# FFN second projection of two layers in float32: the first weight quarter loaded once, the residual loaded seven steps later, eight result sums at other products

## The chip, the cores and the metric

One core of a Trainium2 chip. The metric is device time in microseconds of one execution of the whole program, as the median of three runs. Five engines run beside each other, each through its own instructions in the order in which they were written: TensorE (PE, matmuls; its weight loads are listed as PEld), VectorE (DVE), ScalarE (ACT), GpSimd (POOL) and SyncE (SP). Here SP only starts transfers (DMA), and POOL starts a few more, among them all those that add to their destination. Sixteen DMA engines carry the transfers of both queues.

## The reference

Two layers on 1024 positions of width 1024, float32. The first is a mixer of three branches, the second a mixer with attention followed by a gated MLP with a short convolution. Only the end of that MLP matters here:

```python
z = h @ w_up                       # 1024 x 1024 times 1024 x 5632
...                                # causal convolution of 3 taps over the positions
gate, val = jnp.split(zc, 2, axis=-1)
return (jax.nn.silu(gate) * val) @ w_down      # 1024 x 2816 times 2816 x 1024
```

The result is added to the residual `x` (1024 x 1024), and that is the output.

## The kernel before

All matmuls work on float32 values split into a high and a low part (`hilo`, lines 164 to 166: ScalarE rounds the value to the high part, VectorE subtracts to get the low part); a product of two values is three matmuls (`mm3`, line 206): high by high, high by low, low by high.

The gated activations G lie in memory as 22 tiles of 128 channels by 1024 positions (`G_sp`). The second projection (`down`, from line 1964) multiplies them by `w_dn`, 22 tiles of 128 channels by 1024 outputs. It is written as a 2 x 2 block product with seven products instead of eight. The three dimensions are halved: the positions and the outputs into `lo` and `hi` of 512, the channels into tiles f = 0 to 10 (weights `W1`, G kept in tiles `g11`, `g21` for the two halves of the positions) and 11 to 21 (weights `W2`, G loaded as `g`). The products are numbered 1 to 7 and run in the order 1, 5, 2, 6, 7, 3, 4. Each takes 11 steps, one for each f, so there are 77 units (`units`, line 1970); unit u belongs to product `units[u][0]`. One unit is four blocks of 128 positions (b = 0 to 3) with three matmuls each, accumulated in four PSUM banks. Products 1, 2, 7 and 4 use banks 0 to 3, where 2 adds on 1 and 4 adds on 7; products 5, 6 and 3 use banks 4 to 7.

The left operand x of a unit is one of the G tiles, or S, which holds for each f a running sum of G blocks (one VectorE sum for each unit of products 5, 6 and 3; product 7 forms its sum in `g11`). The right operand y is a quarter of the weights, 128 x 512 for each f, or a sum of quarters in T. T is made by transfers: in product 5 SP loads `W1[:, lo]` into it and POOL starts a transfer that adds `W1[:, hi]` (`more`, line 1975); in products 6 and 4 POOL adds further quarters. Product 7 does the same in six tiles `t3`. For products 1, 2 and 3 the quarter comes into a ring of four tiles `yr`.

The order around this is written out by hand in `step` (line 2105). Before the matmuls of unit u it issues:
- `prep(u + 3)`: the sum, and both splits into `xh`, `xl`, `yh`, `yl`, in rings of four buffers each, so that a preparation needs the buffers that unit u - 1 used;
- `load_sum(u + 9)`: the transfers that make a sum of weights;
- `load(u + 7)`: `yr` for products 1, 2 and 3, and `g` (a ring of twelve tiles in A1) for products 5, 2, 3 and 4;
- in units 13 to 20 one eighth of the residual, `x`, 512 KB;
- in unit 4 of each product, the result tasks of the product before are put into the queue `bgq`; every step takes two tasks from it. A task is one sum on VectorE over 128 x 512 (a copy on ScalarE for product 1) or one store of 128 x 512 to the output.

`opening` (line 1978) runs one slot ahead of the last two slots of the first projection's end and loads G of f = 0 to 3. `rings` (line 1986) runs at that end: it opens the rings, loads units 0 to 6 and prepares 0 to 2. `rest`, in the step of unit 0, loads G of f = 4 to 10 (line 2001) in memory that the first projection used. The last G tile, f = 21, is stored by POOL (line 1909), and POOL's adding transfers come behind that in its queue.

The results of a block b are combined with four output tiles: `t11`, `t12`, `t21`, `t22` are the parts of `x` for the two halves of positions and outputs, `p1` is a copy of product 1, and `w` is product 5 less `p1`, less product 6. In the trace T and x are in tiles named B, S, `g`, `p1` and `w` in tiles named A. All `self.tt` calls are line 159.

Of the kernel before, what the change touches and what calls it, by code (L numbers as in the profile page):

```python
# [106 lines left out]
class Kernel:  # L107
# [1856 lines left out]
    def down(self):  # L1964


        nc, I = self.nc, self.I
        st = {"g": 0}
        half = NF // 2
        units = [(p, f) for p in (1, 5, 2, 6, 7, 3, 4) for f in range(half)]  # L1970
        LOAD, SUM, PREP, LATE = 7, 9, 3, 4
        lo, hi = slice(0, H), slice(H, 2 * H)
        fetch = nc.sync.dma_start

        def more(t, w):
            nc.gpsimd.dma_start(t, w, accum_op=ALU.add)

        def opening():
            st["T"], st["S"] = (self.big(t, F).rearrange("p k (h c) -> p (k h) c", h=2)
                                for t in ("B1", "A0"))  # L1980
            for f in range(4):
                t = st["TS"[f % 2]][:, 12 + f // 2 * 2:14 + f // 2 * 2]
                st["G", f] = t
                fetch(t, self.G_sp[f].rearrange("p (h t) -> p h t", h=2))

        def rings():
            self.right.close()
            self.right = ExitStack()
            st["ring"] = self.right.enter_context(
                self.pool("gd", side="right", reuse_waits="tile"))  # L1990
            for u in range(4):
                load(u)
            for u in range(PREP):
                prep(u)
                load(u + 4)

        def rest():
            self.reopen("cd")
            for f in range(4, half):
                t = st["G", f] = self.c1.tile([P, 2, H], F, name="g%d" % f)  # L2000
                fetch(t, self.G_sp[f].rearrange("p (h t) -> p h t", h=2))
            st["T3"] = [self.c1.tile([P, H], F, name="t3_%d" % i) for i in range(6)]
            st["A1"] = self.big("A1", F, KVN)
            st["p1"] = st["A1"][:, 0:2048].rearrange("p (b c) -> p b c", b=4)
            st["w"] = st["A1"][:, 2048:4096].rearrange("p (b c) -> p b c", b=4)

        def load(u):
            if u >= len(units):
                return
            p, f = units[u]  # L2010
            G2, W1, W2 = self.G_sp[half + f], I["w_dn"][f], I["w_dn"][half + f]
            T, S = st["T"][:, f], st["S"][:, f]
            y = T
            if p == 7:
                y = st["T3"][u % 6]
            elif p in (1, 2, 3):
                y = st["ring"].tile([P, H], F, tag="yr", name="yr", bufs=4)
                fetch(y, {1: W1[:, lo], 2: W2[:, lo], 3: W2[:, hi]}[p])
            g = None
            if p in (5, 2, 3, 4):  # L2020
                st["g"] += 1
                o = 4096 + st["g"] % 12 * H
                g = st["A1"][:, o:o + H]
                fetch(g, G2[:, hi if p in (5, 4) else lo])
            st["in", u] = g, y

        def load_sum(u):

            if u >= len(units):
                return  # L2030
            p, f = units[u]
            W1, W2 = I["w_dn"][f], I["w_dn"][half + f]
            T = st["T"][:, f]
            if p == 5:
                fetch(T, W1[:, lo])
                more(T, W1[:, hi])
            elif p in (6, 4):
                more(T, W2[:, hi if p == 6 else lo])
            elif p == 7:
                t = st["T3"][u % 6]  # L2040
                fetch(t, W1[:, hi])
                more(t, W2[:, hi])

        def prep(u):
            if u >= len(units):
                return
            p, f = units[u]
            g, y = st.pop(("in", u))
            S, (g11, g21) = st["S"][:, f], (st["G", f][:, i] for i in range(2))
            if p == 5:  # L2050
                self.tt(S, g21, g, ALU.subtract)
            elif p == 6:
                self.tt(S, S, g11, ALU.subtract)
            elif p == 7:
                self.tt(g11, g11, g21, ALU.subtract)
            elif p == 3:
                self.tt(S, S, g, ALU.add)
            src = g11 if p in (1, 7) else S if p in (5, 6, 3) else g
            out = []
            for x, n in ((src, "x"), (y, "y")):  # L2060
                t = [st["ring"].tile([P, H], R, tag=n + c, name=n + c, bufs=PREP + 1) for c in "hl"]
                self.hilo(*t, x)
                out.append(t)
            st["op", u] = out

        def macs(u, banks):
            p, f = units[u]
            (xh, xl), (yh, yl) = st["op", u]
            first = f == 0 and p not in (2, 4)
            for b in banks:  # L2070
                ts = slice(b * P, (b + 1) * P)
                self.mm3(st[p][b], (xh[:, ts], xl[:, ts]), (yh, yl), first, f == half - 1,
                         skip_group_check=True)

        def results(p):

            x, tasks = st["x"], []

            def store(t, cs):
                nc.sync.dma_start(self.out[t][:, cs], x[:, t, cs])  # L2080

            for b in range(4):
                ps, p1, w = st[p][b], st["p1"][:, b], st["w"][:, b]
                t11, t12, t21, t22 = x[:, b, lo], x[:, b, hi], x[:, 4 + b, lo], x[:, 4 + b, hi]
                add = lambda o, i, op=ALU.add: tasks.append(lambda: self.tt(o, o, i, op))
                if p == 1:
                    tasks.append(lambda p1=p1, ps=ps: nc.scalar.copy(p1, ps))
                elif p == 5:
                    tasks.append(lambda w=w, ps=ps, p1=p1: self.tt(w, ps, p1, ALU.subtract))
                elif p == 6:  # L2090
                    add(w, ps, ALU.subtract)
                    add(t21, ps)
                    add(t21, p1)
                    add(t12, w)
                    add(t22, w)
                else:
                    o, op, t, cs = {2: (t11, ALU.add, b, lo), 7: (t22, ALU.subtract, 4 + b, hi),
                                    3: (t12, ALU.add, b, hi), 4: (t21, ALU.add, 4 + b, lo)}[p]
                    add(o, ps, op)
                    tasks.append(lambda t=t, cs=cs: store(t, cs))  # L2100
            if p == 6:
                tasks[:] = tasks[0::5] + tasks[1::5] + tasks[2::5] + tasks[3::5] + tasks[4::5]
            return tasks

        def step(u):
            p, f = units[u]

            def pre():
                if u == 0:
                    sets = [self.pair() for _ in range(4)]  # L2110
                    banks = [pr[:, i * H:(i + 1) * H] for pr in sets for i in range(2)]
                    for q in range(1, 8):
                        st[q] = banks[0:4] if q in (1, 2, 7, 4) else banks[4:8]
                    rest()
                prep(u + PREP)
                load_sum(u + SUM)
                load(u + LOAD)
                if u == half + 2:
                    st["x"] = self.big("B0", F)
                if half + 2 <= u < half + 10:  # L2120
                    t = u - half - 2
                    nc.sync.dma_start(st["x"][:, t], self.x2_sp[t])
                if u >= half + LATE and f == LATE:
                    self.bgq.extend(results(units[u - half][0]))
                for _ in range(2):
                    if self.bgq:
                        self.bgq.popleft()()

            def mm():
                if u == len(units) - 2:  # L2130
                    for b in range(4):
                        macs(u, (b,))
                        macs(u + 1, (b,))
                elif u < len(units) - 1:
                    macs(u, range(4))
                else:
                    for task in results(p):
                        task()

            self.slots.append(Slot(pre=pre, mm=mm, name="dn%d.%d" % (p, f)))  # L2140

        self.slots[-2].pre = opening
        self.slots[-1].tail = rings
        for u in range(len(units)):
            step(u)
# [83 lines left out]
```

## Time and profile before

| | us |
|---|---|
| median of 3 runs | 2711.1 (2710.7 to 2712.61) |
| profiled execution | 2704.81 |
| its span, first to last instruction | 2703.0 |
| TensorE busy | 2622.2 |
| VectorE busy | 1881.6 |
| ScalarE busy | 981.1 |
| mean granted TensorE clock | 0.994 of full |

The profile is of one execution. A busy TensorE counts overlapping matmuls, so it says where the engine had work, not how fast it went. All times in the rows are us from the start of the span; the second projection is its last 9%. In a timeline row the bracket at the end is how long the engine was idle before that instruction and what ended the wait. A row such as `xl<-A,xh` reads: written to `xl`, read from A and `xh`.

### The profile page before, as it was taken

How to read it: one execution, taken by the hardware profiler on the slowest of the kernel's cores; microseconds unless marked ns; L12 is line 12 of the kernel's file. 1: busy time of each engine (PE TensorE's matmuls, PEld its weight loads, DVE VectorE, ACT ScalarE, POOL GpSimd, SP SyncE). 2: the span in 40 equal slices, each digit the busy share in tenths (PEclk: the TensorE clock that was granted, in tenths of full speed). 3: DMA queues.
4: the chain of work that ended last, by engine and by line, in shares of the span. 5: the costliest groups of instructions: out<-in, count | busy, mean ns of one | idle time of the engine just before them, and what ended most of it. 6: DMA issues, size and time to landing. Idle time of an engine off the chain costs nothing.

```text
span 2703.0 us, 29526 instructions
## 1 busy us (share of the span) xinstructions
PE 2622.2 (97%) x11688; PEld 2143.6 (79%) x11688; DVE 1881.6 (70%) x2141; ACT 981.1 (36%) x1284; POOL 182.4 (7%) x178
## 2 busy tenths in 40 slices
PE   5999999999999997999999999999999999999998
PEld 3888887888788776877887788888888888887776
DVE  7789988899886664566564254546647788885576
ACT  5322233333343333222243255542323334343333
POOL 4000000000000000000032100000000000000220
PEclk9999999999999998999999999999999999999999
DMA  6111121222232225676342121112532222216964
GB/s 234 55 63 63 63 86 70 102 86 94 86 129 109 99 108 186 255 287 253 125 156 83 68 86 65 68 32 100 180 130 78 86 79 85 88 61 234 276 147 149
DMA packets 102380, 324.63 MB, mean 120 GB/s; under 512 B 11489, under 2 KB 12001, under 8 KB 102242
## 3 DMA queue, kind: packets, MB, share of 16 engines
q1 hardware_dynamic: 95474, 309.65, 31.9%
q0 software_dynamic: 6768, 13.11, 2.6%
q8 instruction: 91, 1.49, 0.2%
q14 instruction: 47, 0.39, 0.0%
HBM read 247.21 MB, written 75.50 MB: 119 GB/s over the span
## 4 chain that ended last, share of the span: by engine, by line
PE 75%; DVE 10%; DMA 7%; ACT 4%; issue 3%; SPq 1%; POOL 1%; DVEq 0%; ACTq 0%; POOLq 0%
PE pp L143 73%; DMA A<-g_sp 1%; DVE h L162 1%; DMA B<-x_sp 1%; DVE sums L159 1%; DVE ld L159 1%; DVE wl L159 1%; DVE A L159 1%; PE pm L143 1%; DVE g L159 1%; DVE B L159 1%; ACT e L156 1%; PE pp L146 1%; PE pm L146 1%; DMA mg_sp<-e 1%
## 5 line engine op out<-in xcount | busy, mean ns | idle before, releaser
L143 PE MATMUL pp<-A,wh 128*128 128x512 f32 x2432 | 769.7, 392 | 13.5 <-DVE A L159 9.0
L143 PEld LDWEIGHTS pp<-A,wh 128*128 128x128 f32 x2432 | 454.4, 188 | 115.1 <-DVE A L159 10.9
L143 PE MATMUL pp<-A,wl 128*128 128x512 f32 x1296 | 506.0, 390 | 2.8 <-DVE wl L159 2.8
L143 PE MATMUL pp<-B,A 128*128 128x512 f32 x1676 | 487.8, 390 | 1.2 <-DVE B L159 1.1
L143 PE MATMUL pp<-A,w 128*128 128x512 f32 x1664 | 443.4, 392 | 12.8 <-DVE pp L159 6.7
L143 PEld LDWEIGHTS pp<-A,w 128*128 128x128 f32 x1664 | 313.7, 189 | 83.3 <-DVE pp L159 10.3
L143 PE MATMUL pp<-B,w 128*128 128x512 f32 x1136 | 374.7, 389 | 0.0
L143 PEld LDWEIGHTS pp<-B,A 128*128 128x128 f32 x1676 | 313.9, 188 | 68.1 <-DVE B L159 2.3
L162 DVE SCALAR_TENSOR_TENSOR h<-p,par_t,h 128x1024 f32<-128x1024 f32 x240 | 312.8, 1303 | 4.7
L143 PEld LDWEIGHTS pp<-A,wl 128*128 128x128 f32 x1296 | 243.8, 188 | 55.4 <-DVE wl L159 4.5
L143 PE MATMUL pp<-B,wh 128*128 128x512 f32 x800 | 263.8, 395 | 15.6 <-ACT B L165 8.3
L159 DVE TENSOR_TENSOR wl<-wr,wh 128x1024 fp32r<-128x1024 f32 (+1 forms) x120 | 144.3, 1203 | 172.7 <-ACT wh L165 168.8
L143 PEld LDWEIGHTS pp<-B,w 128*128 128x128 f32 x1136 | 213.2, 188 | 44.3
L143 PEld LDWEIGHTS pp<-B,wh 128*128 128x128 f32 x800 | 151.3, 190 | 49.3 <-ACT B L165 9.2
L165 ACT CAST wh<-wr 128x1024 fp32r<-128x1024 f32 (+1 forms) x120 | 118.5, 989 | 188.3 <-PE pp L143 159.2
L162 DVE SCALAR_TENSOR_TENSOR z<-pp,par_t,z 128x1023 f32<-128x1023 f32 x88 | 112.6, 1280 | 48.0 <-ACT z L156 47.0
L143 PE MATMUL pp<-yh,xh 128*128 128x512 f32 x308 | 122.6, 398 | 5.9 <-ACT yh L165 5.9
L373 ACT CAST w<-raw 128x1024 fp32r<-128x1024 f32 x50 | 52.6, 1053 | 207.8 <-PE pp L143 141.0
L143 PE MATMUL pp<-yl,xh 128*128 128x512 f32 x308 | 123.1, 400 | 4.4 <-DVE yl L159 4.4
L143 PE MATMUL pp<-A,A 128*128 128x512 f32 x324 | 126.7, 391 | 0.1
L143 PE MATMUL pp<-B,wl 128*128 128x512 f32 x320 | 125.9, 393 | 0.0
L143 PE MATMUL pp<-yh,xl 128*128 128x512 f32 x308 | 121.1, 393 | 0.0
(278 smaller groups left out, 3187.4 us busy)
## 6 DMA issues: line engine op xcount, KB each, us to landing
raw<-in_w_in SPq DMA_DIRECT2D x66, 512.0 KB, 4.1
wr<-in_w_in SPq DMA_DIRECT2D x63, 512.0 KB, 3.5
raw<-in_w_up SPq DMA_DIRECT2D x34, 512.0 KB, 5.2
mg_sp<-e SPq DMA_DIRECT2D x24, 512.0 KB, 4.1
wr<-in_w_br SPq DMA_DIRECT2D x24, 512.0 KB, 5.9
g<-mg_sp SPq DMA_DIRECT2D x24, 512.0 KB, 5.4
A<-g_sp SPq DMA_DIRECT2D x44, 256.0 KB, 6.3
g_sp<-z SPq DMA_DIRECT2D x21, 512.0 KB, 3.0
```

The lines of the kernel that those rows point to most:

```text
L143: return self.nc.tensor.matmul(*a, **k)
L146: self.nc.tensor.transpose(*a)
L156: return self.nc.scalar.activation(out, in_, func, **kw)
L159: return self.nc.vector.tensor_tensor(out, a, b, op)
L162: self.nc.vector.scalar_tensor_tensor(out, a, s, b, op0, op1)
L165: self.nc.scalar.copy(hi, src)
L373: self.nc.scalar.copy(t.__dict__[which][0], src)
```

## The change

- Product 1's quarter `W1[:, lo]` is loaded straight into T, where product 5 needs it too; the ring `yr` now serves products 2 and 3 only, and product 5's second load of the same quarter is gone. Product 5's adding transfer stays.
- The residual is loaded in units 20 to 27 instead of 13 to 20. The tile is still opened in unit 13.
- For each of the four blocks, `t21 += p1` goes from the result tasks of product 6 to those of product 2, and `t12 += w` from those of product 6 to those of product 3. Product 6 has 12 tasks instead of 20, products 2 and 3 have 12 instead of 8. The tasks of products 2 and 6 are reordered, so that the same task of all four blocks comes before the next one; product 3's are not.

```diff
--- before.py
+++ after.py
@@ -2011,11 +2011,13 @@
             G2, W1, W2 = self.G_sp[half + f], I["w_dn"][f], I["w_dn"][half + f]
             T, S = st["T"][:, f], st["S"][:, f]
             y = T
-            if p == 7:
+            if p == 1:
+                fetch(T, W1[:, lo])
+            elif p == 7:
                 y = st["T3"][u % 6]
-            elif p in (1, 2, 3):
+            elif p in (2, 3):
                 y = st["ring"].tile([P, H], F, tag="yr", name="yr", bufs=4)
-                fetch(y, {1: W1[:, lo], 2: W2[:, lo], 3: W2[:, hi]}[p])
+                fetch(y, W2[:, lo if p == 2 else hi])
             g = None
             if p in (5, 2, 3, 4):
                 st["g"] += 1
@@ -2032,7 +2034,6 @@
             W1, W2 = I["w_dn"][f], I["w_dn"][half + f]
             T = st["T"][:, f]
             if p == 5:
-                fetch(T, W1[:, lo])
                 more(T, W1[:, hi])
             elif p in (6, 4):
                 more(T, W2[:, hi if p == 6 else lo])
@@ -2090,16 +2091,18 @@
                 elif p == 6:
                     add(w, ps, ALU.subtract)
                     add(t21, ps)
-                    add(t21, p1)
-                    add(t12, w)
                     add(t22, w)
                 else:
                     o, op, t, cs = {2: (t11, ALU.add, b, lo), 7: (t22, ALU.subtract, 4 + b, hi),
                                     3: (t12, ALU.add, b, hi), 4: (t21, ALU.add, 4 + b, lo)}[p]
+                    if p == 3:
+                        add(o, w)
                     add(o, ps, op)
                     tasks.append(lambda t=t, cs=cs: store(t, cs))
-            if p == 6:
-                tasks[:] = tasks[0::5] + tasks[1::5] + tasks[2::5] + tasks[3::5] + tasks[4::5]
+                    if p == 2:
+                        add(t21, p1)
+            if p in (2, 6):
+                tasks[:] = tasks[0::3] + tasks[1::3] + tasks[2::3]
             return tasks
 
         def step(u):
@@ -2117,8 +2120,8 @@
                 load(u + LOAD)
                 if u == half + 2:
                     st["x"] = self.big("B0", F)
-                if half + 2 <= u < half + 10:
-                    t = u - half - 2
+                if 2 * half - 2 <= u < 2 * half + 6:
+                    t = u - 2 * half + 2
                     nc.sync.dma_start(st["x"][:, t], self.x2_sp[t])
                 if u >= half + LATE and f == LATE:
                     self.bgq.extend(results(units[u - half][0]))
```

## Rows read from the trace of the kernel before

**Rows 1.** The page, section 1: busy us, share of the span, instructions.
```profile
PE 2622.2 (97%) x11688; PEld 2143.6 (79%) x11688; DVE 1881.6 (70%) x2141; ACT 981.1 (36%) x1284; POOL 182.4 (7%) x178
```

**Rows 2.** Tile view, `yh`: duration ns min/median/max, first and last start.
```profile
L143 PE MATMUL pp<-yh,xh x308: 387/389/628, 2467.5 to 2697.8; 128*128 128x512 f32 x154
```

**Rows 3.** Windows: length, busy PE PEld DVE ACT POOL, clock, DMA share, GB/s.
```profile
2467.45:2483.77 16.32, 16.32 (x73) 13.51 (x72) 11.46 (x15) 7.82 (x13) 0.64 (x1) 1.00 0.81 287
2483.77:2490.20 6.43, 6.02 (x25) 4.43 (x24) 3.38 (x6) 3.85 (x7) 1.79 (x2) 1.00 1.05 394
2490.20:2528.28 38.08, 38.08 (x169) 31.53 (x168) 23.17 (x37) 15.76 (x28) 12.42 (x15) 1.00 1.09 297
2528.28:2552.49 24.21, 19.04 (x62) 13.16 (x61) 6.47 (x10) 5.69 (x10) 5.01 (x6) 0.86 1.07 314
2552.49:2625.93 73.44, 73.44 (x325) 60.81 (x324) 55.75 (x90) 30.86 (x54) 14.57 (x17) 1.00 0.63 152
2625.93:2668.60 42.67, 37.96 (x145) 26.16 (x144) 34.28 (x56) 15.70 (x29) 4.70 (x6) 1.00 0.69 182
2668.60:2698.52 29.92, 29.92 (x133) 24.59 (x131) 15.48 (x25) 9.11 (x16) 0.00 (x0) 1.00 0.31 107
```

**Rows 4.** Timeline of ScalarE (start, length, what): unit 7's weight cast.
```profile
2486.17 0.62 ACT L165 CAST yh<-yr 128x512 fp32r<-128x512 f32 x1 [4.36 <-DMA yr<-in_w_dn]
```

**Rows 5.** Timeline of TensorE in product 2: matmuls that had to wait.
```profile
2537.14 0.51 PE L143 MATMUL pp<-yh,xh 128*128 128x512 f32 x1 [1.87 <-ACT yh L165]
...
2547.46 0.50 PE L143 MATMUL pp<-yh,xh 128*128 128x512 f32 x1 [1.35 <-ACT yh L165]
```

**Rows 6.** Timeline of ScalarE in product 2.
```profile
2535.95 0.62 ACT L165 CAST xh<-A 128x512 fp32r<-128x512 f32 x1 [4.31 <-DMA A<-g_sp]
...
2555.37 0.62 ACT L165 CAST xh<-A 128x512 fp32r<-128x512 f32 x1 [0.20 <-PE pp L143]
```

**Rows 7.** Timeline of VectorE, products 7 and 3: `yl`, result adds.
```profile
2648.95 0.69 DVE L159 TENSOR_TENSOR yl<-yr,yh 128x512 fp32r<-128x512 f32 x1
2649.55 1.29 DVE L159 TENSOR_TENSOR B<-B,A 128x512 f32<-128x512 f32 x2
...
2652.81 0.69 DVE L159 TENSOR_TENSOR yl<-yr,yh 128x512 fp32r<-128x512 f32 x1
...
2655.47 0.68 DVE L159 TENSOR_TENSOR yl<-yr,yh 128x512 fp32r<-128x512 f32 x1
...
2658.72 0.68 DVE L159 TENSOR_TENSOR yl<-yr,yh 128x512 fp32r<-128x512 f32 x1
```

**Rows 8.** Timeline of VectorE: `yl` of units 40 and 70.
```profile
2582.56 0.68 DVE L159 TENSOR_TENSOR yl<-B,yh 128x512 fp32r<-128x512 f32 x1
...
2672.56 0.69 DVE L159 TENSOR_TENSOR yl<-B,yh 128x512 fp32r<-128x512 f32 x1
```

**Rows 9.** DMA issues 2477.5 to 2555: queue, count, KB, us to landing.
```profile
B<-in_w_dn POOLq DMA_DIRECT2D x22, 256.0 KB, 7.3
A<-g_sp SPq DMA_DIRECT2D x21, 256.0 KB, 12.2
B<-x_sp SPq DMA_DIRECT2D x8, 512.0 KB, 13.9
yr<-in_w_dn SPq DMA_DIRECT2D x13, 256.0 KB, 10.6
B<-in_w_dn SPq DMA_DIRECT2D x11, 256.0 KB, 9.2
```

**Rows 10.** Timeline of SyncE's queue at the start of the stage.
```profile
2457.06 13.28 SPq L2018 DMA_DIRECT2D yr<-in_w_dn  x7
2470.38 5.16 SPq L2001 DMA_DIRECT2D g<-g_sp  x7
```

**Rows 11.** Timeline of GpSimd: first and 22nd accumulating transfer.
```profile
2488.05 1.90 POOL L1976 DMA_DIRECT2D B<-in_w_dn  x2 [13.03 <-ACT yh L165]
...
2541.51 0.86 POOL L1976 DMA_DIRECT2D B<-in_w_dn  x1 [1.24 <-issue]
```

## The prediction

> **What bounds the kernel now.** I read the page first: TensorE (PE) is busy for 97% of the span [rows 1], so anything that is gained must be a place where PE waits or runs slowly inside the second FFN projection, the only code that the diff touches. The tile view gives that stage its length: 308 first-of-three matmuls, four to a unit, so 77 units of twelve matmuls, from 2467.5 us [rows 2]. I call the start of unit u T(u). Next I cut the stage into stretches [rows 3]. From 2490.20 to 2528.28 PE is busy all the time and does 14 units in 38.08 us: 2.72 us a unit, at full clock. At that pace 77 units take 209.4 us; they take 231.07 (the sum of the stretches). The 21.6 us that are lost lie in three stretches only:
> - 2483.77 to 2490.20: two units in 6.43 us instead of 5.44, **0.99 us lost**. ScalarE stood 4.36 us for a weight quarter `yr` of unit 7 [rows 4].
> - 2528.28 to 2552.49: five units (22 to 26, product 2) in 24.21 instead of 13.60, **10.61 us lost**.
> - 2625.93 to 2668.60: twelve units (54 to 65, the end of product 7 and all of product 3) in 42.67 instead of 32.64, **10.03 us lost**.
>
> Everywhere else PE runs at 2.72, so there no edit can gain anything.
>
> The 10.61 us are the DMA's. PE waits for the cast `yh` [rows 5], and ScalarE stands idle before its cast `xh` for a transfer `A<-g_sp`, 4.31 us in a cycle of 5.4 [rows 6]. The 16 engines are over 100% busy from 2483.77 to 2552.49 [rows 3]. The granted clock is 0.86 there, so PE is for part of it at the lower level of 1.2 GHz; as the data set the pace, that costs nothing further, and the clock is back at 1.00 in the next stretch.
>
> The 10.03 us are VectorE's (DVE). Its loop per unit there is: one sum, then (after ScalarE's cast) `xl`, then `yl`, then the result adds that this step hands out. From `yl` to `yl` this takes 3.86 us with two adds, 2.66 with none, 3.25 with one [rows 7]: against PE's 2.72 a step with two adds falls back by 1.14, one with one add by 0.53, one with none wins 0.06. The operands are made three units ahead, which gives a lead: `yl` of unit 40 ends at 2583.24, and T(40) is 2552.49 + 13 x 2.72 = 2587.85, a lead of 4.6 us. For unit 70 it is 2679.48 - 2673.25 = 6.2 us, and that is the most that four buffers give [rows 8]. Check: from step 37 on, before has four steps with one add (product 2's), seven with none, ten with two (product 6's twenty adds), one with none, three with one (product 7's; its fourth falls to product 4's short preparation): 2.1 - 0.4 + 11.4 - 0.1 + 1.6 = 14.6; less the lead of 4.6 it is 10.0, which is what was lost.
>
> **The change, part by part.** *The first quarter loaded once.* Eleven transfers of 256 KB on SP go (the `B<-in_w_dn` of SP [rows 9]); product 1's now land in T. A transfer costs 0.262 MB / 297 GB/s = 0.88 us while accumulating transfers run beside it, and 0.67 at 394 GB/s in the stretch where few do [rows 3]: 7.4 to 9.7 us of DMA time are saved. Two things move with it. (a) SP's loads 0 to 6 took 13.28 us, because a ring of four `yr` buffers held them, and the seven G loads stood behind them until 2470.38 [rows 10]; into T they need no ring, so G starts up to 10 us sooner. I take this as full for six of the seven. The last one may be held to about 2475 as now by the memory it reuses; that it isn't would gain nothing more. Unit 7's quarter then finds nothing but that one in front of it, and the 0.99 us go. (b) GpSimd (POOL) no longer waits for a fetch before product 5's eleven accumulations. They ran from 2488.05; they may now run from about 2475, after POOL's store of the last G, each once product 1 has read its slot, and product 6's eleven, which went until 2541.51 [rows 11], may run from T(8) on, the last from T(18) + 1.95 = 2518.4 (1.95 us is what a preparation takes after its buffers come free: 8.16 - 6.2). The yr ring leaves the start of its pool, so xh to yl lie on other memory than before: PE might find unit 0's operands late, between 0 and 1.4 us (a cast and a difference by the DVE and ACT rows of such shapes, 0.62 + 0.69). I take 0: four tiles lie on the old weight buffers either way.
>
> *The residual seven steps later.* Eight transfers of 512 KB leave steps 13 to 20, where they stood before product 2's loads, for steps 20 to 27. Before: the transfers issued from 2477.5 to 2555 are 22 accumulations, 21 g, 13 yr, 11 quarters and the residual's 16 halves, 83 x 0.88 = 73 of 77.5 us [rows 9]; that is why product 2's g come late. After, from 2475 to T(19) + 1.95 = 2521, where yr of unit 26 must wait for its buffer and SP with everything behind it: one G (2), four quarters, 11 g of product 5, four yr and four g of product 2 (25), and 22 accumulations: 47 x 0.88 = 41.4 us, done at 2516. Units 22 to 25 have their data. (Where data are there, ScalarE waits for PE's buffers, as at 2555.37 [rows 6].) From 2521 unit 32's g is the 24th of the 256 KB transfers, with the residual between: 2521 + 24 x 0.88 = 2542, while its preparation starts at T(29) = 2546.3 at the earliest. So PE doesn't stop in product 2, **10.61 us go**, and product 6 starts with the full lead of 6.2 instead of the 4.6 that was left of it. The residual is first read at step 37, T = 2568; its last piece lands near 2550.
>
> *The adds.* No add is gone. Four `t21 += p1` go from product 6's results to product 2's, four `t12 += w` to product 3's. Product 2's results are now 4 adds (steps 37, 38), 4 stores (39, 40), 4 adds (41, 42); product 6's are twelve adds, steps 48 to 53. Sum of fallbacks: 2.28 - 0.12 + 2.28 - 0.3 + 6.84 - 0.3 + 1.6 = 12.3; less the lead of 6.2, 6.1 us are lost instead of 10.0: **3.9 us gained** (2.4 if the lead stays at 4.6). Product 3's eight adds come at steps 70 to 75 beside product 4's preparation, which has no sum; DVE is busy 15.48 of 29.92 us there [rows 3]. Four adds of 0.6 more are hidden; without that cover they would cost 2.4. The stores on SP block only loads that have six steps to spare.
>
> **Sum.** 0.99 + 10.61 + 3.9 = 15.5 us. The profiled execution took 2704.81 us, its span 2703.0; the median of the timed runs is 2711.1, 6.3 us above. One trace doesn't show where executions differ; I take the 15.5, made against the profiled one, off the median unchanged: **2695.6 us**. The three gains add, because each is a delay of PE against its own pace and DVE, the DMA and PE meet again with a full lead in between.
>
> **Rivals.** *A, the residual crowds the second half of product 2.* It shares steps 20 to 25 with two loads a step. Where accumulations of product 6 are still queued at 2521, SP's pace is that of before, 77.5 us for its 61 transfers, 1.27 us: unit 32's g is there at 2521 + 24 x 1.27 = 2551.5, PE just doesn't stop, but the lead is 1.0 instead of 6.2, and DVE's stretch loses 11.3: gain 11.6 - 1.3 = 10.3, 2700.8 us. For it: the full steps. Against it: POOL can be done at 2520. *B, product 3's loads take DVE's place*, since DVE goes through its steps faster: only the 11.6 stay, 2699.5 us. For it: DMA is at 0.69 over that stretch [rows 3]; against it: 0.31 of 42.67 us is 13 us that the engines have free, and DVE's stretch gets 3.9 shorter. *C, POOL's burst starves product 1.* If memory holds all seven G loads to 2470.4 as now, and POOL's accumulations come at 2475 all at once, 18 transfers of SP (seven G of two, four quarters) stand against them. Five are done by 2475. At SP's 1.27 us the other 13 are in by 2491.5, in time for T(10) - 1.95 = 2492.7, at no cost. If POOL gets one transfer in for each of SP's, they take 2 x 0.88 = 1.76 us, the last lands at 2497.9, 5.2 us late, and PE stands in product 1: gain 10.3, 2700.8 us. For it: POOL did run its 22 as soon as it might [rows 11]; against it: SP had 61 of the 83 [rows 9].
>
> That second case is a rule of the Trainium skill ("DMA: Bandwidth & Descriptors", section "Queues, rings and completion order"): each DMA engine takes the queues that have work in turn, a packet at a time, which speaks against letting POOL's accumulations out early. No row here shows single packets; over the whole stretch the shares of rows 9 are not half and half.
>
> *D, slower.* The same place, POOL's early queue, but SP held back through product 5 as well: its 25 transfers between 2475 and T(22) = 2527.3 have 2.1 us each; from (52.3 + 15.5) / 25 = 2.7 us each on, all that is gained is gone. At 3.0 us they need 75 us: 22.7 lost, 7.2 slower, 2718 us. Against it: 1.27 is the worst pace that the trace has with the same 22 accumulations.
>
> **How the numbers follow.** Forecast 0.64, its own range 2694 to 2698 (lead 4.6 to 6.2, first unit 0 to 1.4). A 0.14, B 0.07, C 0.07, D 0.03, and 0.05 that product 2's stall moves on to units 27 to 32 with most of its size (gain 5 or less). Faster by over 0.2% (5.4 us, about what timing can tell here) is the first four: 0.92; within 0.2%: 0.05; slower 0.03. The range goes from 2693.5 to the end of A and C, 2702.
>
> **What would show it.** Right: PE busy without a gap and at clock 1.00 from 2467 to about T(50); ScalarE's waits for `A<-g_sp` gone; POOL's first accumulation near 2475, its 22nd by 2525; residual transfers after 2520; the loop of 3.86 us for product 6's results six times, and PE's loss between units 52 and 66 near 6 us. Wrong: PE idle before unit 7 (C), a residual that meets `A<-g_sp` waits at units 27 to 32 (A), ScalarE waiting for yr or g in product 3 (B).

## The result and the profile after

The changed kernel takes 2693.98 us (median of four runs, 2693.33 to 2698.93) against 2711.3 for the kernel before (2710.7 to 2712.61) beside it: ratio 0.9939, 95% interval [0.9922, 0.9957], 17.3 us. The forecast was 2695.6, in a range from 2693.5 to 2702.0.

The profiled execution took 2694.05 us, its span 2692.3. The stage of 77 units starts at 2472.10 in it. Windows of the changed kernel, cut where PE's pace changes (length, busy PE PEld DVE ACT POOL, granted clock, DMA share, GB/s), to be held against [rows 3]:

```profile
2472.10:2616.26 144.16, 144.16 (x637) 119.37 (x636) 99.84 (x156) 61.31 (x107) 32.16 (x37) 1.00 0.84 225
2616.26:2634.61 18.35, 16.15 (x61) 10.87 (x60) 14.53 (x25) 5.71 (x10) 6.97 (x8) 1.00 0.97 181
2634.61:2648.22 13.61, 13.61 (x62) 11.26 (x60) 9.79 (x16) 5.71 (x10) 0.00 (x0) 1.00 0.76 255
2648.22:2657.64 9.42, 8.96 (x37) 6.52 (x36) 7.89 (x14) 5.44 (x11) 0.00 (x0) 1.00 0.49 150
2657.64:2687.56 29.92, 29.92 (x133) 24.59 (x131) 18.14 (x29) 9.11 (x16) 0.00 (x0) 1.00 0.32 107
```

Units 0 to 52 run at 2.72 us each without a gap (144.16 / 53). Units 53 to 57 lose 18.35 - 13.60 = 4.75 us, 63 to 65 lose 9.42 - 8.16 = 1.26. Unit 7's stall is gone, product 2's stall is gone, and products 7 and 3 lose 6.02 us instead of 10.03. In all, the stage loses 6.02 us instead of 21.63: **15.6 us less, where 15.5 were forecast**.

In product 2 ScalarE no longer waits for `A<-g_sp` as in [rows 6] but for PE to release its buffers, as it should where data are early. ScalarE in product 2:

```profile
2545.51 0.62 ACT L165 CAST xh<-A 128x512 fp32r<-128x512 f32 x1 [1.58 <-PE pp L143]
```

SyncE's queue of the changed kernel, against [rows 10]:

```profile
2461.70 3.68 SPq L2015 DMA_DIRECT2D B<-in_w_dn  x7
2465.49 12.69 SPq L2001 DMA_DIRECT2D g<-g_sp  x7
2478.23 2.66 SPq L2015 DMA_DIRECT2D B<-in_w_dn  x4
...
2529.63 0.62 SPq L2125 DMA_DIRECT2D B<-x_sp  x1
...
2542.99 2.28 SPq L2125 DMA_DIRECT2D B<-x_sp  x3
```

Seven quarters go out in 3.68 us instead of 13.28, and G follows them at 2465.49, 6.6 us ahead of the first matmul (before: 2.9 us after it). The seven take until 2478.2: one of them is held, as was assumed. The residual goes out between 2529.63 and 2545.3. GpSimd's accumulating transfers, first and 22nd, against [rows 11]:

```profile
2478.74 2.76 POOL L1976 DMA_DIRECT2D B<-in_w_dn  x3
...
2526.75 0.86 POOL L1976 DMA_DIRECT2D B<-in_w_dn  x1 [0.99 <-DVE yl L159]
```

The first three start 6.6 us into the stage (before: 20.6), the last is 54.7 us into it (before: 74.1). VectorE, `yl` of unit 40, and a cycle with two sums while it prepares product 3, against [rows 7, 8]:

```profile
2574.02 0.68 DVE L159 TENSOR_TENSOR yl<-B,yh 128x512 fp32r<-128x512 f32 x1
...
2623.49 0.69 DVE L159 TENSOR_TENSOR yl<-yr,yh 128x512 fp32r<-128x512 f32 x1
2624.09 1.28 DVE L159 TENSOR_TENSOR B<-B,A 128x512 f32<-128x512 f32 x2
...
2627.35 0.68 DVE L159 TENSOR_TENSOR yl<-yr,yh 128x512 fp32r<-128x512 f32 x1
```

The cycle is the same 3.86 us (2623.49 to 2627.35). What differs is the lead: `yl` of unit 40 ends at 2574.70, and unit 40 starts at 2472.10 + 40 x 2.72 = 2580.90, 6.2 us later instead of 4.6.

The two profiled executions differ by 10.8 us and not by 15.6, because the stage begins 4.65 us later in that of the changed kernel. The code ahead of it is the same in both. Most of the difference arises at the end of the first layer; smaller differences elsewhere go both ways. Window 1000 to 1100 us of the kernel before, then of the changed one:

```profile
1000.00:1100.00 100.00, 82.87 (x335) 64.58 (x334) 48.49 (x72) 34.41 (x35) 1.46 (x3) 0.91 0.50 182
```

```profile
1000.00:1100.00 100.00, 83.07 (x314) 63.66 (x313) 45.02 (x54) 34.40 (x35) 1.46 (x3) 0.88 0.47 172
```

The changed kernel does 21 matmuls fewer there, at a granted clock of 0.88 instead of 0.91; at 2.72 / 12 = 0.227 us each these are 4.8 us. In the twelve further kernels below, with the same code there, the stage begins between 2467.7 and 2477.4 us. So executions of the same code differ by some 10 us before the change is reached, and the part of 17.3 us that is more than 15.6 can't be told from that. What follows is judged by the loss inside the stage, which the trace gives to a few tenths: length of the stage less 77 x 2.72 = 209.44.

### The profile page after: what moved, and what is told of

It reads as the page before. It is cut to its first block, busy times and chain, and to the rows that moved or that the text cites. A ratio compares the mean times of both kernels' runs of the same rounds, so it can differ in the third digit from the quotient of the medians.

```text
span 2692.3 us, 29507 instructions
## 1 busy us (share of the span) xinstructions
PE 2619.1 (97%) x11688; PEld 2145.2 (80%) x11688; DVE 1881.0 (70%) x2141; ACT 980.9 (36%) x1284; POOL 182.2 (7%) x178
## 4 chain that ended last, share of the span: by engine, by line
PE 78%; DVE 9%; DMA 5%; ACT 3%; issue 3%; SPq 1%; POOL 1%; ACTq 0%; DVEq 0%; POOLq 0%
PE pp L143 76%; DMA ld<-h_sp 1%; DVE h L162 1%; DVE sums L159 1%; DVE A L159 1%; DVE g L159 1%; PE pm L143 1%; ACT e L156 1%; DVE wl L159 1%; PE pp L146 1%; PE pm L146 1%; DMA wr<-in_w_out 1%; DMA mg_sp<-e 1%; DVE B L159 1%; DVE ld L159 0%
## 5 line engine op out<-in xcount | busy, mean ns | idle before, releaser
L143 PEld LDWEIGHTS pp<-A,wh 128*128 128x128 f32 x2432 | 454.5, 188 | 115.0 <-DVE A L159 10.8
```

Of the source, the lines that this page charges most:

```text
L143: return self.nc.tensor.matmul(*a, **k)
```

## The experiments

Theory: PE loses only what the DMA or VectorE makes it wait; product 2's stall goes with the transfers ahead of it, and products 6, 7 and 3 lose the sum of their fallbacks (about 0.6 us a sum) less the lead at product 6, which is called the law below. Rivals: the residual's place alone, the bytes alone, or the sums alone do it. First each part alone, then pairs. All ratios are to the kernel before, timed beside each. The last four columns are the us that PE loses in these products.

| kernel | ratio, 95% interval | product 1 | product 2 | products 6 to 3 | sum |
|---|---|---|---|---|---|
| before | | 0.99 | 10.61 | 10.03 | 21.63 |
| changed | 0.9939 [0.9922, 0.9957] | 0 | 0 | 6.02 | 6.02 |
| quarter | 0.9953 [0.9935, 0.9971] | 0 | 0 | 8.42 | 8.42 |
| residual | 0.998 [0.997, 0.999] | 1.61 | 0.79 | 14.03 | 16.43 |
| sums | 0.9994 [0.9984, 1.0004] | 1.78 | 9.48 | 8.12 | 19.38 |
| quarter, residual | 0.9956 [0.9942, 0.9971] | 0 | 0 | 8.43 | 8.43 |
| quarter, sums | 0.9942 [0.9927, 0.9957] | 0 | 0 | 6.02 | 6.02 |
| residual, sums | 0.9956 [0.9941, 0.9971] | 0.59 | 0.05 | 11.56 | 12.20 |

**The quarter alone.**

```diff
+            if p == 1:
+                fetch(T, W1[:, lo])
...
-            elif p in (1, 2, 3):
+            elif p in (2, 3):
...
             if p == 5:
-                fetch(T, W1[:, lo])
                 more(T, W1[:, hi])
```

> Only the first part: product 1's quarter goes into T and isn't loaded again for product 5; residual and sums as before. Theory (transfers counted one by one, lead and fallbacks): from the start of the stage to the step where SP must wait for the yr ring there are 25 + 12 of SP's 256 KB pieces and 22 accumulations, 59 x 0.88 = 52 us, which ends close to that step, so product 2 isn't starved; product 7 and 3 lose 14.6 - 6.2 = 8.4 us because the lead is full and the sums are where they were. Loss of PE in the stage 8.4 us instead of 21.6. Rival (the residual's place ahead of product 2's loads is what starves it, whatever the bytes): a stall of 2 us or more stays in units 22 to 32 and the lead stays near 4.6, a loss of 12 us or more.

Windows of product 2 and of products 6 to 3:

```profile
2531.17:2561.09 29.92, 29.92 (x133) 24.78 (x132) 18.75 (x30) 12.55 (x22) 3.25 (x4) 1.00 0.80 232
2561.09:2659.27 98.18, 94.32 (x397) 73.59 (x396) 75.13 (x122) 37.41 (x67) 16.56 (x19) 1.00 0.66 165
```

Product 2 takes 29.92 us, eleven units at full pace, with the residual where it always was; the second window is 98.18 - 89.76 = 8.42 over. That is the theory's number to the tenth, and the rival falls.

**The residual alone.**

```diff
-                if half + 2 <= u < half + 10:
-                    t = u - half - 2
+                if 2 * half - 2 <= u < 2 * half + 6:
+                    t = u - 2 * half + 2
```

> Only the second part: the residual in steps 20 to 27; the quarter is loaded twice, sums as before. Theory: 33 of SP's 256 KB pieces and 22 accumulations before the yr ring holds SP, 48 us, which is done in time, so product 2 isn't starved; the 0.99 us at unit 7 stay; the lead is full or up to 1 us short: 0.99 + 8.4 to 9.4, a loss of 9.4 to 10.4 us. Rival (bytes are what counts, the residual only moves its collision): 5 us or more lost in units 27 to 32.

Windows of units 0 to 8, of product 2 and of products 6 to 3:

```profile
2471.97:2498.06 26.09, 25.05 (x109) 20.20 (x108) 16.79 (x24) 12.29 (x21) 3.31 (x4) 1.00 0.91 315
2533.42:2564.13 30.71, 30.48 (x134) 24.63 (x132) 14.85 (x24) 10.28 (x18) 4.35 (x5) 1.00 1.02 324
2564.13:2667.92 103.79, 97.31 (x397) 73.10 (x396) 79.34 (x128) 39.70 (x71) 19.23 (x22) 1.00 0.66 164
```

In all 16.4 us are lost, and neither side had it: product 2 hardly stops (0.79), yet products 6 to 3 lose 14.03. GpSimd's last accumulation of product 6, then ScalarE's longest wait, then `yl` of unit 40:

```profile
2544.77 0.86 POOL L1976 DMA_DIRECT2D B<-in_w_dn  x1 [1.11 <-issue]
```

```profile
2551.09 0.62 ACT L165 CAST xh<-A 128x512 fp32r<-128x512 f32 x1 [5.14 <-DMA A<-g_sp]
```

```profile
2581.84 0.68 DVE L159 TENSOR_TENSOR yl<-B,yh 128x512 fp32r<-128x512 f32 x1
```

The 22nd accumulation goes out 72.8 us into the stage, amid the residual. ScalarE then stands 5.14 us for a g, and unit 40 is ready at 2582.52 for a start at 2564.13 + 7 x 2.72 = 2583.17: a lead of 0.65 us. The law then says 14.6 - 0.65 = 13.95; 14.03 are lost. My count for this kernel was wrong at one point: it took all 22 accumulations as done when the residual starts, while with the quarter loaded twice POOL must wait for each second load. This is rival A of the prediction, in the kernel where POOL is late.

**The sums alone** (`t21 += p1` to product 2's results, `t12 += w` to product 3's, as in the change).

> Only the third part: the sums moved, transfers as before. Theory: 0.99 and 10.61 us stay, and the end of product 7 and product 3 lose 12.3 - 4.6 = 7.7 instead of 10.0: a loss of 19.3 us, 2.3 gained. Rival (the gain there came from the full lead, the moved sums only change places): 21.6.

```profile
2531.32:2570.72 39.40, 33.86 (x133) 25.53 (x132) 19.45 (x31) 14.01 (x25) 9.22 (x11) 0.96 1.00 282
2570.72:2668.60 97.88, 94.36 (x398) 73.57 (x396) 74.62 (x120) 38.25 (x69) 14.82 (x17) 1.00 0.62 157
```

The windows are product 2 and products 6 to 3. The DMA's stall stays (39.40 - 29.92 = 9.48), the other falls from 10.03 to 8.12. In all 19.38 us are lost, against 19.3 by the theory. The moved sums are worth about 2 us by themselves; the timing, at 0.9994, can't tell that from none.

**Pairs.** The edits are those above.

> The first and second part, the sums as before. Theory (once the quarter is loaded once the residual's place is free of cost, and the lead is full either way): the same as with the quarter alone, 8.4 us lost. Rival (the residual's move gains something that the moved sums hide): 7.5 or less.

> The first and third part, the residual at its old steps 13 to 20. Theory (with the quarter alone PE lost 8.42 us, so product 2 has its data in time wherever the residual stands, and the moved sums take 2.3 off that): 6.1 us lost, as in the changed kernel with all three. Rival (the residual's move keeps something back that shows only beside the others): 7 us or more.

> The second and third part, the quarter loaded twice. Theory (with the residual alone PE lost 16.4 us: POOL's accumulations come late, are still queued beside the residual, and eat the lead before product 6; the moved sums take 2.3 off): 14.1 us lost. Rival (the sums and the residual's place are enough): 8 us or less.

Windows: of quarter and residual, products 6 to 3; of quarter and sums, the whole stage; of residual and sums, units 0 to 8, product 2, products 6 to 3.

```profile
2567.05:2665.24 98.19, 94.20 (x397) 73.55 (x396) 75.12 (x121) 37.41 (x67) 16.56 (x19) 1.00 0.66 165
```

```profile
2471.24:2686.70 215.46, 212.71 (x925) 172.60 (x923) 150.10 (x236) 87.34 (x153) 39.10 (x45) 1.00 0.75 204
```

```profile
2467.71:2492.78 25.07, 24.84 (x109) 20.20 (x108) 16.79 (x24) 12.29 (x21) 3.30 (x4) 1.00 0.90 322
2528.14:2558.11 29.97, 29.97 (x133) 24.75 (x132) 14.89 (x24) 10.28 (x18) 4.35 (x5) 1.00 1.07 345
2558.11:2659.43 101.32, 95.99 (x398) 73.30 (x396) 76.87 (x124) 39.68 (x71) 19.24 (x22) 1.00 0.67 165
```

Beside the quarter the residual's move gains nothing: 8.43 with it and 8.42 without, 6.02 (215.46 - 209.44) without and 6.02 with it when the sums are moved too. Without the quarter the lead is nearly gone: 11.56, and 12.2 in all, nearer to the theory's 14.1 than to the rival's 8. Of the 1.9 us between 14.1 and 12.2, 1.76 lie in products 1 and 2 (0.64 lost, against 2.40 with the residual alone), where these two kernels do the same. So much can executions differ where the DMA sets the pace; where it doesn't, they agree to a few hundredths (8.42 and 8.43, 6.02 twice).

**What the quarter's part does it by.** It saves bytes, and it starts transfers early. The first kernel is the changed one with the bytes put back:

```diff
             if p == 5:
+                fetch(st["ring"].tile([P, H], F, tag="yr", name="yr", bufs=4), W1[:, lo])
                 more(T, W1[:, hi])
```

> The changed kernel plus eleven loads of 256 KB that nothing reads: product 5's quarter once more into a yr tile, at the step where it was loaded before. So the bytes are those of before, but POOL's accumulations don't wait for the loads. Theory E (the accumulations' early start is what counts): SP's 36 pieces and 22 accumulations take 51 us and are in 5 us after SP is held at the yr ring; product 2 isn't starved, the lead is 5 to 6.2, a loss of 6 to 7.5 us. Theory B (the bytes count): the lead is gone before product 6 as with the residual alone, a loss of 11 us or more.

Windows of product 2 and of products 6 to 3, and GpSimd's first and 22nd accumulation:

```profile
2528.36:2558.28 29.92, 29.92 (x134) 24.78 (x132) 19.10 (x31) 13.71 (x24) 2.95 (x4) 1.00 1.01 345
2558.28:2655.16 96.88, 93.58 (x398) 73.64 (x396) 73.95 (x120) 37.41 (x67) 16.27 (x19) 1.00 0.66 166
```

```profile
2475.15 2.76 POOL L1976 DMA_DIRECT2D B<-in_w_dn  x3
...
2527.21 0.86 POOL L1976 DMA_DIRECT2D B<-in_w_dn  x1 [1.74 <-DVE xl L159]
```

7.12 us are lost, ratio 0.9934 [0.992, 0.9949]. The kernel with residual and sums moved has the same bytes, the same place of the residual and the same sums, but not the early start, and loses 12.20; the changed kernel loses 6.02. So beside the other two parts the quarter is worth 6.18 us: about 5 by the early start and about 1 by the bytes, by one trace each. How the 13.21 us of the quarter alone divide was not run. The early start has two halves: SP is no longer held at the ring, and POOL no longer waits for a second load. The next kernel keeps SP's hold and the bytes, and lets POOL start early:

```diff
             if p == 1:
                 fetch(T, W1[:, lo])
+                y = st["ring"].tile([P, H], F, tag="yr", name="yr", bufs=4)
+                fetch(y, W1[:, lo])
```

> The changed kernel, but product 1 takes its quarter from the ring of four as before, and a second load of the same quarter goes into T right ahead of it. So the bytes and SP's hold at the ring are those of before, and only POOL's accumulations start early. Theory E1 (POOL's early start alone is what counts): product 2 isn't starved and the lead at product 6 is 5 to 6.2: 6.0 to 7.3 us lost in products 6 to 3, beside 1 to 5 us in product 1, where the loads are late. Rival E2 (SP's early loads are what counts): the lead is gone before product 6, 11 us or more lost in products 6 to 3.

Windows of units 0 to 8, product 2 and products 6 to 3; GpSimd's first accumulations, ScalarE's cast for unit 7, and the window between these two:

```profile
2471.08:2503.91 32.83, 26.63 (x109) 21.33 (x108) 15.22 (x21) 11.23 (x19) 9.48 (x11) 0.90 0.99 292
2539.27:2569.19 29.92, 29.92 (x133) 24.77 (x132) 19.22 (x31) 12.53 (x22) 3.55 (x4) 1.00 0.98 333
2569.19:2665.01 95.82, 93.06 (x398) 73.69 (x396) 72.74 (x117) 37.42 (x67) 15.68 (x18) 1.00 0.65 164
```

```profile
2478.65 2.76 POOL L1976 DMA_DIRECT2D B<-in_w_dn  x3
```

```profile
2495.81 0.62 ACT L165 CAST yh<-yr 128x512 fp32r<-128x512 f32 x1 [9.87 <-DMA yr<-in_w_dn]
```

```profile
2478.65:2495.81 17.16, 11.63 (x52) 9.30 (x50) 4.84 (x8) 4.05 (x8) 5.37 (x7) 0.93 1.06 330
```

Products 6 to 3 lose 6.06, as in the changed kernel (6.02), but product 1 loses 32.83 - 24.48 = 8.35, where 1 to 5 were expected: ScalarE waits 9.87 us for unit 7's quarter, and the clock falls to 0.90 in that stretch. That is 14.41 us in all, no less than the 12.20 with the same bytes and POOL late, at a ratio of 0.9973 [0.996, 0.9985]. This is the mechanism of rival C, POOL's early transfers against SP's late ones, but no test of its 5.2 us: C had no second loads between SP's late ones. The transfers were not slower than the prediction priced them either: 330 GB/s in the last window, against the 297 [rows 3] behind its 0.88 us. The stall also gives the DMA 8 us more ahead of product 2, so this run doesn't show what POOL's early start alone would do there; that stays open. What it shows is that POOL's early start without SP's moves the loss to product 1, where the four kernels with SP held and POOL late lose 0.59 to 1.78.

**The lead.** It differs between the kernels above. `yl` of unit 40 with the sums alone, with residual and sums, and with the bytes put back:

```profile
2584.96 0.68 DVE L159 TENSOR_TENSOR yl<-B,yh 128x512 fp32r<-128x512 f32 x1
```

```profile
2575.80 0.68 DVE L159 TENSOR_TENSOR yl<-B,yh 128x512 fp32r<-128x512 f32 x1
```

```profile
2571.52 0.68 DVE L159 TENSOR_TENSOR yl<-B,yh 128x512 fp32r<-128x512 f32 x1
```

Against the start of unit 40 (7 x 2.72 us behind that of product 6's window) these are leads of 4.1, 0.7 and 5.1 us. By the law 8.2, 11.6 and 7.2 us are lost then; 8.12, 11.56 and 7.12 were.

The next kernels shorten the lead on purpose: two units ahead instead of three, in two versions. In the first, product 7's sums of weights are overwritten before they are read, so part of the result is changed; its instructions are as many.

```diff
-        LOAD, SUM, PREP, LATE = 7, 9, 3, 4
+        LOAD, SUM, PREP, LATE = 7, 9, 2, 4
...
+            for u in range(PREP + 4, LOAD):
+                load(u)
```

> The changed kernel with operands made two units ahead instead of three and rings of three buffers instead of four. Theory (the lead is what the sums of the results use up): the full lead is 2 x 2.72 - 1.95 = 3.5 us instead of 6.2, so 12.3 - 3.5 = 8.8 us are lost in products 7 and 3 instead of 6.0. Rival (VectorE's work in the stretch sets the loss, whatever the lead): 6.0.

Window of products 6 to 3, and a cast of ScalarE for product 7:

```profile
2564.22:2665.65 101.43, 95.42 (x397) 73.40 (x396) 75.03 (x120) 37.60 (x67) 15.69 (x18) 1.00 0.65 164
```

```profile
2594.99 0.62 ACT L165 CAST yh<-t 128x512 fp32r<-128x512 f32 x1 [2.35 <-DMA t<-in_w_dn]
```

Products 6 to 3 lose 11.67 us, ratio 0.9966 [0.9955, 0.9977]. In this loss is a wait of 2.35 us for a transfer into a tile that was taken over too soon, so it doesn't test the lead by itself. The second version has all three distances shorter (`6, 8, 2, 4`):

> The changed kernel with operands made two units ahead, loads six and sums of weights eight units ahead, rings of three. Theory (the lead is what the result sums use up): a full lead of 2 x 2.72 - 1.95 = 3.5 us, so 12.3 - 3.5 = 8.8 us lost from product 6 on, and up to 1 us at the third unit. Rival (VectorE's work in the stretch sets the loss, whatever the lead): 6.0.

Windows of units 0 to 8 and of products 6 to 3, and `yl` of unit 39:

```profile
2477.37:2502.88 25.51, 24.78 (x109) 20.19 (x108) 16.47 (x23) 11.37 (x19) 7.73 (x9) 1.00 0.99 291
2568.16:2667.22 99.06, 94.89 (x397) 73.47 (x396) 74.96 (x120) 37.50 (x67) 15.69 (x18) 1.00 0.66 164
```

```profile
2580.33 0.68 DVE L159 TENSOR_TENSOR yl<-B,yh 128x512 fp32r<-128x512 f32 x1
```

`yl` of unit 39 ends at 2581.01, the unit starts at 2568.16 + 6 x 2.72 = 2584.48: a lead of 3.47 us, where 3.5 was reckoned. 99.06 - 89.76 = 9.3 us are lost, against 8.8 by the theory and 6.0 by the rival; another 1.03 at unit 2. The 0.5 between 8.8 and 9.3 is a term that the count left out: with two units ahead all four of product 7's sums delay units of product 3 (0.53 us each), and not only three. Units 62 to 65 of this kernel:

```profile
2654.54:2667.22 12.68, 12.03 (x49) 8.70 (x48) 10.12 (x17) 5.54 (x11) 0.00 (x0) 1.00 0.70 205
```

They lose 12.68 - 10.88 = 1.80 us, where 63 to 65 of the changed kernel lose 1.26. Ratio 0.9963 [0.995, 0.9977].

**Sums where VectorE has time.** The changed kernel with `t21 += p1` and `t22 += w` and its store at product 3's results as well:

```diff
                     add(w, ps, ALU.subtract)
                     add(t21, ps)
-                    add(t22, w)
...
                     add(o, ps, op)
-                    tasks.append(lambda t=t, cs=cs: store(t, cs))
-                    if p == 2:
+                    if p != 7:
+                        tasks.append(lambda t=t, cs=cs: store(t, cs))
+                    if p == 3:
+                        add(t22, w)
+                        tasks.append(lambda b=b: store(4 + b, hi))
                         add(t21, p1)
             if p in (2, 6):
-                tasks[:] = tasks[0::3] + tasks[1::3] + tasks[2::3]
+                tasks[:] = tasks[0::2] + tasks[1::2]
...
-                for _ in range(2):
+                for _ in range(2 if u < 6 * half else 4):
```

> The changed kernel, but all sums that have time go to product 3's results: t21 += p1 and t22 += w with its store too, and four result tasks a step from product 4 on. Product 2 keeps four sums, product 6 eight, product 7 four. Theory: fallbacks 2.28 - 0.12 - 0.4 + 4.56 - 0.4 + 2.28 = 8.2, less the lead of 6.2: a loss of 2.0 us instead of 6.0, and product 4 hides sixteen sums. Rival (sums beside product 4 aren't hidden, or the stores at the end delay the last ones): no gain over the changed kernel, PE loses at units 70 to 76 or the tail grows by 2 us or more.

Windows of products 6 to 3 and of product 4, and VectorE's sum for a unit of product 3:

```profile
2561.93:2654.37 92.44, 91.29 (x398) 74.05 (x396) 68.68 (x110) 37.43 (x67) 14.83 (x17) 1.00 0.67 173
2654.37:2684.29 29.92, 29.92 (x133) 24.59 (x131) 22.11 (x36) 9.11 (x16) 0.00 (x0) 1.00 0.22 83
```

```profile
2633.18 0.69 DVE L159 TENSOR_TENSOR A<-A,A 128x512 f32<-128x512 f32 x1 [0.69 <-DMA A<-g_sp]
```

2.68 us are lost where 2.0 were expected, and the 0.7 between them is VectorE's wait for one g, 0.69 us. Product 4, with VectorE busy 22.11 of 29.92 us, still runs at 2.72 a unit. The kernel takes 2689.58 us, ratio 0.9926 [0.9908, 0.9944]. Then also product 7's four sums four steps later:

```diff
-                if u >= half + LATE and f == LATE:
+                if u >= half and f == (8 if units[u - half][0] == 7 else LATE):
```

> As the kernel with the late sums (all that have time at product 3's results), and product 7's four sums from PSUM four steps later, at steps 63 and 64, beside product 4's short preparation. Theory: fallbacks 2.28 - 0.12 - 0.4 + 4.56 - 0.7 = 5.6 us, under the lead of 6.2: 0 to 0.7 us lost (the kernel with the late sums lost 0.7 more than counted), so 5.3 to 6.0 less than the changed kernel. Rival (the lead isn't all usable, or product 4 must wait for the bank that product 7's sums read): 2 us or more lost, at units 60 to 66.

Windows as above, and PE at unit 66:

```profile
2564.73:2655.10 90.37, 90.31 (x397) 74.09 (x396) 66.63 (x107) 37.41 (x67) 14.81 (x17) 1.00 0.69 178
2655.10:2685.63 30.53, 30.22 (x133) 24.52 (x131) 24.14 (x39) 9.11 (x16) 0.00 (x0) 1.00 0.22 82
```

```profile
2656.94 0.50 PE L143 MATMUL pp<-yh,xh 128*128 128x512 f32 x1 [0.31 <-DVE B L159]
```

0.61 us are lost in products 6 to 3, and another 0.61 at unit 66, where PE waits for the bank that product 7's sums still read. That is 1.2 us in all, and the stage is 4.8 us better than in the changed kernel. The kernel takes 2689.78 us, ratio 0.9926 [0.9914, 0.9938]. By the trace it is the best version here; by the timing alone it can't be told from the one before it.

## Why the prediction was right, step by step

- **Unit 7, 0.99 us to 0**: right, and for the reason given: G goes out before the stage begins.
- **Product 2, 10.61 us to 0**: right in size, but the account of it is only half right. The prediction credits it to the residual's later place, the early transfers of (a) and (b) and the saved bytes together. In the runs either the quarter or the residual's move takes the stall away: nothing is left of it with the quarter alone, 0.79 us with the residual alone. What only the quarter does is to keep the lead for product 6, 6.2 us against 0.65. Beside the quarter the residual's move gains nothing (8.43 against 8.42, 6.02 against 6.02). Of the quarter's worth beside the other two parts the early start is about 5 us and the bytes about 1. The count of 47 transfers was too early as well: it has them done at 2516, while its own last accumulation may start only at 2518.4. In the trace that one goes out 54.7 us into the stage, at 2522.1 on the prediction's clock. The stall went all the same, so in this term the right size was partly luck.
- **Products 7 and 3, 10.03 us to 6.1**: 6.02 measured. The lead of 6.2 is in the trace, and so is the fallback of 1.14 us a step with two sums. With each kernel's own lead, from 0.65 to 6.2 us, the law gives what is lost to 0.1 us in the ten kernels from the one before to the one with the ring kept. Where it missed by more, a term was left out: the fourth sum of product 7 with two units ahead, and the wait for a g with the late sums.
- **Unit 0 on other memory, 0 to 1.4 us**: 0 measured; PE goes from the last matmul of the first projection to unit 0 without a gap.
- **The sums hidden beside product 4**: right, and eight more could hide there.
- **Rivals.** A is real where POOL is late: the residual alone leaves a lead of 0.65 us where A had reckoned 1.0. C's mechanism is real where SP stays held: 8.35 us, with second loads in the queue that C did not have. Neither came, because the early SP and the early POOL come together in one edit. B didn't come: in product 3 PE waits for VectorE's chain only. It shows, with 0.69 us, once fewer sums hold VectorE up. Nothing of D is in the trace.
- **The median**: taking the stage's gain off the median of before gave 1.6 us too much time, which is within what executions differ ahead of the stage.

## What to carry to other kernels

Where an engine works just slower than the one it feeds, its lead is what counts: work out the fallback of each step and the lead at the start of the stretch, and the loss follows, here to a tenth of a microsecond; sums are best put beside a step that has no other work for that engine. When a transfer is saved, ask first which other transfers waited for it: here, beside the other two parts, the early start of two queues was worth about 5 us and the bytes about 1. And take an edit of several parts apart: one of these three gains nothing beside the others.

## What the runs showed of the hardware that was not expected

A stretch that the change doesn't touch differs between executions by several microseconds: 335 against 314 matmuls in 100 us at a granted clock of 0.91 and 0.88, and starts of the last stage from 2467.5 to 2477.4 us. And a transfer that comes late need not be a slow one: where ScalarE stood 9.87 us for unit 7's quarter, the DMA moved 330 GB/s, more than the 297 at which the prediction priced its transfers. The quarter had more transfers ahead of it and beside it.
